# The sums of the LayerNorm behind depthwise convolutions, moved from GpSimd to VectorE in a two-layer hybrid backbone

## Chip, cores and metric

The kernel runs on 1 core of one Trainium2 chip. The metric is the device time of one execution in microseconds, from the first to the last instruction with what lies around them; several executions are taken and the median is shown. The profile is of one further execution.

## What is computed

Two layers, each with three branches over 1024 latent tokens and 256 context tokens of width 1024: windowed attention, a Conformer convolution, and a bidirectional gated recurrence. Every branch is gated, projected, merged and normalised. The change touches the convolution branch and, by a reservation of buffers, the attention. Cut to these:

```python
def layer_norm(x):
    mu = jnp.mean(x, -1, keepdims=True)
    var = jnp.mean(jnp.square(x - mu), -1, keepdims=True)
    return (x - mu) * lax.rsqrt(var + LN_EPS)

def conformer_conv(u, dw_w, dw_b, ln_g, ln_b):
    a, g = jnp.split(u, 2, axis=-1)
    y = a * jax.nn.sigmoid(g)
    y = depthwise_conv(y, dw_w, dw_b, (15, 15))      # 31 taps, one filter per channel, 512 channels
    y = layer_norm(y) * ln_g + ln_b                  # over the 512 channels
    return jax.nn.silu(y)
```

In attention, queries of a block of 128 tokens see their own and the neighbouring blocks of keys and the 256 context keys, with a learned sink per head.

## The kernel before

Channels lie on the 128 partitions and tokens along the free axis, so 512 channels are four tiles. Each layer has a first phase (`phase1`, line 525) with projections, convolution, recurrence and attention, and a second (`phase2`, line 1150) with the branch projections, the merge and the output. All large matrices are split into a rounded part and a remainder (hi and lo, as whi and wlo, ph and pl, qh and ql): ScalarE writes the first, VectorE the second, and TensorE multiplies three of the four combinations or, in attention, two.

The first phase is written as nine generators (line 1135): lru, att_values, att_scores, lru_in, lru_out, att_proj, att_out, conv and gates. A planner (class `Driver`, line 105) runs them in the order of estimated ready times and a priority table (line 44). It keeps its own clocks for TensorE, ScalarE and VectorE: every instruction given to these engines passes a `Meter` (line 52) that adds an estimated cost. GpSimd and the DMA queues have no clock in it. A generator yields the engine that its next step belongs to, an earliest time, and conditions such as room in a pool of buffers: `sl` holds 10 full-size slots, `hl_` 14 half-size tiles of 512 columns, `pl_` the use of PSUM. A step whose condition fails isn't taken. The gate projections (`gate_nt`, line 1093) need one tile of `hl_` for each step; they are long runs of matmuls that wait for nothing but weights and room, and so fill TensorE between steps of the others. The emitted program is put into each engine's queue by the framework's scheduler; on the chip each queue runs in order.

The convolution (`conv`, line 761) makes four accumulators of 31 taps each on VectorE and parks three of them in DRAM. Then, for each group of columns (layer 0: 256 context columns, 512, 512; layer 1: 512, 512), it loads them back (ab and acc2, line 804), adds the four tiles up on GpSimd into sm (lines 810 and 812), and sums over partitions with a matmul by a matrix of ones (line 816). VectorE subtracts the mean in place with four instructions that read that PSUM tile (line 820), ScalarE squares (line 824), GpSimd adds the squares up into sq (line 829), and a second matmul by ones gives the variance (line 831); root, reciprocal, scaling and the swish follow.

Attention is `att_scores` (line 945) and `att_values` (line 1034). For a block of 128 tokens and four heads, qh and ql are multiplied by the keys into PSUM; VectorE reads this with mask and maximum into P (in profiles CUSTOM_DVE_ANT_0, in the order ISA), ScalarE exponentiates, VectorE scales by the inverse sums es. TensorE transposes P in fours into pt, ScalarE and VectorE split pt into ph and pl, and two value products yp read these. A queue in order means that a value product on pl, and all matmuls behind it, wait until VectorE has come to that pl.

In `att_scores` the buffers of qh and ql are reserved (line 962) behind a yield that can pass control to other generators:

```python
yield ("act", hl_.room(3), at["proj"][2 * kv + 1])
qs[i] = load_q(kv, tl)
yield ("act", drv_.t["pe"] + LAG_Q[l])
...
hl_.take(2)
```

Of the kernel before, what the change touches and what calls it, by code (L numbers as in the profile page):

```python
# [12 lines left out]
ALU = mybir.AluOpType  # L13
# [176 lines left out]
def kernel(  # L190
# [7 lines left out]
    pool, sp = nc.gpsimd, nc.sync  # L198
    pe, act, dve = Meter(nc.tensor, pe_cost), Meter(nc.scalar, act_cost), Meter(nc.vector, dve_cost)
# [22 lines left out]
    def psum(n=512, name="ps"):  # L222
        return PM.tile([128, n], F32, tag="mm", name=name, bufs=4)
# [122 lines left out]
    def wroom(n=1):  # L346
        return lambda: wlive[0] + n <= NW

    def wcols(src, o):
        return Wt(src[:, o:o + 128].rearrange("(k p) n -> p k n", p=128), KD, 128)  # L350
# [171 lines left out]
    def both(*conds):  # L522
        return lambda: all(c() for c in conds)

    def phase1(l, R, RH):
# [5 lines left out]
        sl, hl_, pl_ = Pool_(NS), Pool_(NHF), Pool_(4)  # L531
        state = dict(lru=False, late=False)

        def slot(name, dt=F32):
            return R.tile([128, SLOT], dt, tag="s", name=name, bufs=NS)

        def half(name, dt=F32):
            return RH.tile([128, 512], dt, tag="h", name=name, bufs=NHF)
# [222 lines left out]
        def conv():  # L761
            for cc in range(4):
                yield ("pe", both(wroom(), sl.room(2)))
                sl.take(2)
                wg = wcols(w_in[l], O_U + BW + cc * 128)
                u = slot("u")
                if not last:
                    pool.memset(u[:, 0:15], 0.0)
                pool.memset(u[:, 15 + C:UL], 0.0)
                pool.memset(u[:, UL + S:UL + S + 15], 0.0)  # L770
                uo = lambda nt: u[:, 15:15 + C] if nt[0] == 0 else u[:, UL + nt[1] - C:UL + nt[1] - C + nt[2]]

                def evac_g(ps, nt):
                    act.activation(out=uo(nt), in_=ps, func=AF.Tanh, scale=0.5)

                def evac_a(ps, nt):
                    dve.scalar_tensor_tensor(out=uo(nt), in0=uo(nt), scalar=1.0, in1=ps, op0=ALU.add, op1=ALU.mult)

                for nt in full:
                    yield from gemm_nt(wg, nt, evac_g)  # L780
                wg.free()
                yield ("pe", wroom())
                wa = wcols(w_in[l], O_U + cc * 128)
                for nt in full:
                    yield from gemm_nt(wa, nt, evac_a)
                wa.free()
                acc = slot("acc")
                tap = lambda k: cwt[l][:, k * 4 + cc:k * 4 + cc + 1]
                yield "dve"
                dve.tensor_scalar(out=acc[:, QA:QE], in0=u[:, QA:QE], scalar1=tap(0),  # L790
                                  scalar2=p[:, P_CB + cc:P_CB + cc + 1], op0=ALU.mult, op1=ALU.add)
                for k in range(1, CK):
                    dve.scalar_tensor_tensor(out=acc[:, QA:QE], in0=u[:, QA + k:QE + k], scalar=tap(k),
                                             in1=acc[:, QA:QE], op0=ALU.mult, op1=ALU.add)
                    if k % 2 == 0 and k < CK - 1:
                        yield "dve"
                if cc < 3:
                    sp.dma_start(out=acc_d[cc][:, QA:QE], in_=acc[:, QA:QE])
                    sl.give(2)
            for nt in full:  # L800
                o, n = 0 if nt[0] == 0 else QL + nt[1] - C, nt[2]
                yield ("act", hl_.room(LH))
                hl_.take(LH)
                ab, a2 = slot("ab"), half("acc2")
                accs = [ab[:, 0:n], ab[:, 512:512 + n], a2[:, 0:n], acc[:, o:o + n]]
                for cc in range(3):
                    sp.dma_start(out=accs[cc], in_=acc_d[cc][:, o:o + n])
                yield ("dve", max(drv_.t["pe"], drv_.t["dve"]) + LAG_CONV[l])
                rstd, sm = half("rstd")[:, 0:n], half("sm")[:, 0:n]
                pool.tensor_tensor(out=sm, in0=accs[0], in1=accs[1], op=ALU.add)  # L810
                for cc in (2, 3):
                    pool.tensor_tensor(out=sm, in0=sm, in1=accs[cc], op=ALU.add)
                yield ("pe", lambda: pl_.used < 3)
                pl_.take()
                ps = psum()
                pe.matmul(out=ps[:, 0:n], lhsT=ones_f, rhs=sm, start=True, stop=True)
                sm = None
                for cc in range(4):
                    yield "dve"
                    dve.scalar_tensor_tensor(out=accs[cc], in0=ps[:, 0:n], scalar=-1.0 / BW, in1=accs[cc], op0=ALU.mult,  # L820
                                             op1=ALU.add)
                    yield "act"
                    sq = half("sq")[:, 0:n]
                    act.activation(out=sq, in_=accs[cc], func=AF.Square)
                    if sm is None:
                        sm = sq
                    else:
                        yield "dve"
                        pool.tensor_tensor(out=sm, in0=sm, in1=sq, op=ALU.add)
                yield "pe"  # L830
                pe.matmul(out=ps[:, 0:n], lhsT=ones_f, rhs=sm, start=True, stop=True)
                yield "act"
                act.activation(out=rstd, in_=ps[:, 0:n], func=AF.Sqrt, scale=1.0 / BW, bias=epsc)
                pl_.give()
                yield "dve"
                dve.reciprocal(out=rstd, in_=rstd)
                for cc in range(4):
                    yield "dve"
                    v = accs[cc]
                    dve.tensor_tensor(out=v, in0=v, in1=rstd, op=ALU.mult)  # L840
                    yield "act"
                    th = half("thc")[:, 0:n]
                    act.activation(out=th, in_=v, func=AF.Tanh, scale=d[:, 40 + cc:41 + cc], bias=d[:, 44 + cc:45 + cc])
                    act.activation(out=v, in_=v, func=AF.Identity, scale=p[:, P_CG + cc:P_CG + cc + 1],
                                   bias=p[:, P_CLB + cc:P_CLB + cc + 1])
                    yield "dve"
                    dve.scalar_tensor_tensor(out=v, in0=th, scalar=1.0, in1=v, op0=ALU.add, op1=ALU.mult)
                    sp.dma_start(out=acc_d[cc][:, o:o + n], in_=v)
                hl_.give(LH)
            sl.give(2)  # L850

            def get(nt):
                o, n = 0 if nt[0] == 0 else QL + nt[1] - C, nt[2]
                y = half("yc")
                sp.dma_start(out=y[:, 0:n], in_=acc_d[cc][:, o:o + n])
                return y[:, 0:n]

            for cc in range(4):
                yield from gating(1, cc, get, 0.5)
# [76 lines left out]
        def load_q(kv, tl):  # L936
            hl_.take()
            qd = half("qd")
            q3 = qd.rearrange("p (h t) -> p h t", t=128)
            for dh in range(2):  # L940
                sp.dma_start(out=q3[64 * dh:64 * dh + 64], in_=q_d[kv * 256:kv * 256 + 256, tl * 128:tl * 128 + 128].rearrange(
                    "(h p) t -> p h t", p=64))
            return qd

        def att_scores():

            qs = {}
            for i, (kv, tl) in enumerate(blocks):
# [7 lines left out]
                if i not in qs:  # L956
                    yield ("act", hl_.room(3), at["proj"][2 * kv + 1])
                    qs[i] = load_q(kv, tl)
                    yield ("act", drv_.t["pe"] + LAG_Q[l])
                else:  # L960
                    yield ("act", hl_.room(2))
                hl_.take(2)
                ks = at["ks"][kv]
                qh, ql = half("qh", F32R), half("ql", F32R)
                split(qs.pop(i), qh, ql)
# [139 lines left out]
        def gates():  # L1105
# [27 lines left out]
            assert not todo  # L1133

        drv_.run([lru(), att_values(), att_scores(), lru_in(), lru_out(), att_proj(), att_out(), conv(), gates()], PRIO[l])
        assert wlive[0] == 0 and sl.used == 0 and hl_.used == 0 and pl_.used == 0

# [334 lines left out]
```

## Time and profile before

| | |
|---|---|
| median of 3 runs | 2308.1 us (2306.67 to 2308.55) |
| the profiled execution | 2302.58 us |
| its span, first to last instruction | 2300.8 us |
| mean granted TensorE clock | 0.991 |
| TensorE busy | 2246.2 us (98%) |
| VectorE busy | 1681.3 us (73%) |
| ScalarE busy | 1004.4 us (44%) |
| GpSimd busy | 86.0 us (4%) |

In the profile PE is TensorE's matmuls, PEld its weight loads, DVE is VectorE, ACT ScalarE, POOL GpSimd and SP SyncE, which issues most DMAs. All instructions to metered engines are recorded by one line, 73, so they are told apart by their tiles: out<-in. A timeline row gives start, duration, engine and instruction, and in brackets how long the engine stood idle before it and what it waited for. Durations of neighbours overlap; the distance from one start to the next is what an instruction costs its queue.

### The profile page before, as it was taken

How to read it: one execution, taken by the hardware profiler on the slowest of the kernel's cores; microseconds unless marked ns; L12 is line 12 of the kernel's file. 1: busy time of each engine (PE TensorE's matmuls, PEld its weight loads, DVE VectorE, ACT ScalarE, POOL GpSimd, SP SyncE). 2: the span in 40 equal slices, each digit the busy share in tenths (PEclk: the TensorE clock that was granted, in tenths of full speed). 3: DMA queues.
4: the chain of work that ended last, by engine and by line, in shares of the span. 5: the costliest groups of instructions: out<-in, count | busy, mean ns of one | idle time of the engine just before them, and what ended most of it. 6: DMA issues, size and time to landing. Idle time of an engine off the chain costs nothing.

```text
span 2300.8 us, 29975 instructions
## 1 busy us (share of the span) xinstructions
PE 2246.2 (98%) x11344; PEld 1870.3 (81%) x11344; DVE 1681.3 (73%) x2453; ACT 1004.4 (44%) x1642; POOL 86.0 (4%) x140
## 2 busy tenths in 40 slices
PE   7999999999999999999999999999999999999998
PEld 2888888888888887888888788888888878878886
DVE  5579967868959875544678749879778797755767
ACT  4555563245444575421132544665243446642110
POOL 1000000000000111000001100000000011000002
PEclk8999999999999999999999999999999999999999
DMA  7223323433334232555561312224433234337532
GB/s 277 76 74 101 115 74 126 143 111 110 98 109 140 80 117 88 191 167 174 147 220 65 103 55 79 76 82 139 136 96 106 83 115 134 123 132 228 162 126 92
DMA packets 270945, 279.90 MB, mean 122 GB/s; under 512 B 19768, under 2 KB 199888, under 8 KB 270800
## 3 DMA queue, kind: packets, MB, share of 16 engines
q1 hardware_dynamic: 242288, 226.06, 31.5%
q10 hardware_dynamic: 28512, 51.92, 6.4%
q8 instruction: 89, 1.46, 0.3%
q14 instruction: 56, 0.46, 0.1%
HBM read 203.04 MB, written 74.88 MB: 121 GB/s over the span
## 4 chain that ended last, share of the span: by engine, by line
PE 91%; DVE 3%; ACT 3%; DMA 2%; issue 1%; POOLq 0%; SPq 0%; POOL 0%; DVEq 0%; ACTq 0%
PE ps L73 84%; PE yp L73 3%; PE pt L73 2%; PE pa L73 1%; ACT whi L73 0%; DMA raw<-in_w_ada_dram 0%; DVE acc L73 0%; DVE wlo L73 0%; DVE pl L73 0%; DVE P L73 0%; PE p L73 0%; DVE xp L73 0%; DMA raw<-in_w_in_dram 0%; ACT hf L73 0%; DMA yst<-yd 0%
## 5 line engine op out<-in xcount | busy, mean ns | idle before, releaser
L73 PE MATMUL ps<-hlhi,whi 128*128 128x512 f32 x1728 | 681.0, 395 | 2.8 <-DVE pl L73 1.5
L73 PE MATMUL ps<-hllo,whi 128*128 128x512 f32 x1728 | 677.2, 392 | 0.0
L73 PE MATMUL ps<-hlhi,wlo 128*128 128x512 f32 x1728 | 676.6, 392 | 0.0
L73 PEld LDWEIGHTS ps<-hlhi,wlo 128*128 128x128 f32 x1728 | 325.5, 188 | 67.8 <-issue 0.4
L73 PEld LDWEIGHTS ps<-hlhi,whi 128*128 128x128 f32 x1728 | 326.2, 189 | 66.6 <-DVE pl L73 2.8
L73 PEld LDWEIGHTS ps<-hllo,whi 128*128 128x128 f32 x1728 | 326.0, 189 | 61.8 <-issue 0.2
L73 DVE SCALAR_TENSOR_TENSOR acc<-u,cwt,acc 128x1296 f32<-128x1296 f32 (+1 forms) x240 | 341.8, 1424 | 2.2
L73 ACT ACTIVATE whi<-raw 128x1024 fp32r<-128x1024 f32 x180 | 190.1, 1058 | 336.7 <-PE ps L73 303.0
L73 DVE TENSOR_TENSOR wlo<-raw,whi 128x1024 fp32r<-128x1024 f32 x180 | 220.5, 1225 | 97.4 <-ACT whi L73 94.3
L73 PE MATMUL ps<-yy,whi 128*128 128x512 f32 (+1 forms) x960 | 271.5, 368 | 2.2 <-DVE m L73 2.2
L73 PEld LDWEIGHTS ps<-yy,whi 128*128 128x128 f32 x960 | 173.7, 188 | 32.7 <-DVE m L73 2.4
L73 PE MATMUL ps<-yy,wlo 128*128 128x512 f32 (+1 forms) x480 | 176.5, 368 | 0.0
L73 ACT ACTIVATE ph<-pt 128x512 fp32r<-128x512 f32 x160 | 94.2, 593 | 140.2 <-PE pt L73 138.4
L73 DVE TENSOR_TENSOR pl<-pt,ph 128x512 fp32r<-128x512 f32 x160 | 109.3, 686 | 54.5 <-ACT ph L73 52.9
L73 PE MATMUL ps<-hchi,whi 128*128 128x256 f32 x480 | 135.9, 283 | 1.2 <-DVE pl L73 0.4
L73 PE MATMUL ps<-hchi,wlo 128*128 128x256 f32 x480 | 135.5, 282 | 1.0 <-DVE wlo L73 1.0
L73 ACT ACTIVATE P<-P,nm 128x640 f32<-128x640 f32 (+1 forms) x128 | 101.9, 798 | 75.2 <-DVE nm L73 74.9
L73 PE MATMUL ps<-hclo,whi 128*128 128x256 f32 x480 | 134.7, 281 | 0.0
L73 DVE CUSTOM_DVE_ANT_0 P<-ps,m_mid,nsink 128x640 f32<-128x640 f32 (+1 forms) x112 | 93.4, 859 | 42.6 <-PE ps L73 41.1
L73 ACT ACTIVATE tg<-ps,drv 128x512 f32<-128x512 f32 (+1 forms) x120 | 76.5, 638 | 69.0 <-PE ps L73 68.4
L73 PEld LDWEIGHTS ps<-yy,wlo 128*128 128x128 f32 x480 | 90.5, 188 | 15.1
L73 PE MATMUL pt<-ident,P 128*128 128x128 f32 x640 | 97.5, 273 | 2.9 <-DVE pl L73 1.4
(205 smaller groups left out, 3397.9 us busy)
## 6 DMA issues: line engine op xcount, KB each, us to landing
raw<-in_w_in_dram SPq DMA_DIRECT2D x60, 512.0 KB
raw<-in_w_ada_dram SPq DMA_DIRECT2D x48, 512.0 KB
raw<-in_w_gate_dram SPq DMA_DIRECT2D x48, 512.0 KB
th<-tg ACTq DMA_DIRECT2D x96, 256.0 KB
thl<-th SPq DMA_DIRECT2D x96, 256.0 KB
yd<-gs ACTq DMA_DIRECT2D x48, 256.0 KB
yst<-yd SPq DMA_DIRECT2D x48, 256.0 KB
raw<-in_w_branch_dram SPq DMA_DIRECT2D x24, 512.0 KB
```

What stands on the lines that cost most here:

```text
L73: return f(*a, **k)
```

## The change

The three adds of the accumulators and the three adds of squares of each group are issued on VectorE instead of GpSimd. VectorE's instructions are metered, so the planner's clock for VectorE now counts them. In att_scores the two half-size buffers are reserved before the wait behind the load of queries, no longer after it.

```diff
--- before.py
+++ after.py
@@ -807,9 +807,9 @@
                     sp.dma_start(out=accs[cc], in_=acc_d[cc][:, o:o + n])
                 yield ("dve", max(drv_.t["pe"], drv_.t["dve"]) + LAG_CONV[l])
                 rstd, sm = half("rstd")[:, 0:n], half("sm")[:, 0:n]
-                pool.tensor_tensor(out=sm, in0=accs[0], in1=accs[1], op=ALU.add)
+                dve.tensor_tensor(out=sm, in0=accs[0], in1=accs[1], op=ALU.add)
                 for cc in (2, 3):
-                    pool.tensor_tensor(out=sm, in0=sm, in1=accs[cc], op=ALU.add)
+                    dve.tensor_tensor(out=sm, in0=sm, in1=accs[cc], op=ALU.add)
                 yield ("pe", lambda: pl_.used < 3)
                 pl_.take()
                 ps = psum()
@@ -826,7 +826,7 @@
                         sm = sq
                     else:
                         yield "dve"
-                        pool.tensor_tensor(out=sm, in0=sm, in1=sq, op=ALU.add)
+                        dve.tensor_tensor(out=sm, in0=sm, in1=sq, op=ALU.add)
                 yield "pe"
                 pe.matmul(out=ps[:, 0:n], lhsT=ones_f, rhs=sm, start=True, stop=True)
                 yield "act"
@@ -956,10 +956,11 @@
                 if i not in qs:
                     yield ("act", hl_.room(3), at["proj"][2 * kv + 1])
                     qs[i] = load_q(kv, tl)
+                    hl_.take(2)
                     yield ("act", drv_.t["pe"] + LAG_Q[l])
                 else:
                     yield ("act", hl_.room(2))
-                hl_.take(2)
+                    hl_.take(2)
                 ks = at["ks"][kv]
                 qh, ql = half("qh", F32R), half("ql", F32R)
                 split(qs.pop(i), qh, ql)
```

The change moves instructions, because the planner chooses anew from the first of these adds on. Up to there TensorE's order is the same. `ps<-sm,ones_f` is the matmul of the sums, `hlhi`, `hllo`, `whi` and `wlo` make projections, `pt` transposes, `ks` scores, `yp` value products.

TensorE, layer 0, around the second group's sum, before:

```order
L73 MATMUL ps<-hlhi,wlo 128x512
L73 MATMUL yp<-ph,vs 128x512
L73 MATMUL yp<-pl,vs 128x512
L73 MATMUL ps<-sm,ones_f 128x512
L73 MATMUL yp<-ph,vs 128x512
L73 MATMUL yp<-pl,vs 128x512
L73 MATMUL ps<-hlhi,whi 128x512
```

Here 19 projection matmuls follow in a row. With the change, the same place:

```order
L73 MATMUL ps<-hlhi,wlo 128x512
L73 MATMUL ps<-sm,ones_f 128x512
L73 MATMUL pt<-ident,P 128x128 x4
L73 MATMUL ps_7800<-ks,qh 128x384
L73 MATMUL ps_7800<-ks,ql 128x384
L73 MATMUL ps_7800<-ks,qh 128x256
L73 MATMUL ps_7800<-ks,ql 128x256
L73 MATMUL ps_7806<-ks,qh 128x384
L73 MATMUL ps_7806<-ks,ql 128x384
L73 MATMUL ps_7806<-ks,qh 128x256
L73 MATMUL ps_7806<-ks,ql 128x256
L73 MATMUL pt<-ident,P 128x128 x4
```

Behind it stand three more rounds of two value products and four transposes, eight scores on the next queries and a value product, and only then projections again. The projections between the sum and the attention's steps have moved.

VectorE, the same place with the change, directly behind the four subtractions of the mean (sq is the add of squares):

```order
L73 ISA P,nm_7713<-ps_7800,m_mid,nsink 128x640
L73 ISA nm_7713 128x1
L73 ISA P,nm_7713<-ps_7806,m_mid,nsink 128x640
L73 ISA nm_7713 128x1
L73 TENSOR_TENSOR pl<-pt,ph 128x512 x2
L73 TENSOR_TENSOR sq<-sq 128x512
L73 TENSOR_TENSOR es<-nm_7713,sink 128x4
L73 TENSOR_TENSOR pl<-pt,ph 128x512
L73 TENSOR_TENSOR es<-es,sm_7715 128x4
L73 RECIPROCAL es<-es 128x4
L73 TENSOR_SCALAR P<-P,es 128x640 x3
L73 TENSOR_TENSOR ql<-qd,qh 128x512
```

All pl that the value products read, and the ql that the next scores read, stand behind the subtractions and the two conversions to P; an add of squares stands between them.

TensorE, layer 1, around the second group's sum, before:

```order
L73 MATMUL yp<-ph,vs 128x512
L73 MATMUL yp<-pl,vs 128x512
L73 MATMUL ps<-sm,ones_f 128x512
L73 MATMUL yp<-ph,vs 128x512
L73 MATMUL ps_16659<-ks,qh 128x384
L73 MATMUL ps_16659<-ks,ql 128x384
L73 MATMUL ps_16659<-ks,qh 128x256
L73 MATMUL ps_16659<-ks,ql 128x256
L73 MATMUL ps<-hlhi,whi 128x512
```

Here 14 projection matmuls follow. With the change:

```order
L73 MATMUL ps<-hlhi,whi 128x512
L73 MATMUL ps<-sm,ones_f 128x512
L73 MATMUL pt<-ident,P 128x128 x4
L73 MATMUL ps<-hllo,whi 128x512
L73 MATMUL ps<-hlhi,wlo 128x512
L73 MATMUL ps<-hlhi,whi 128x512
L73 MATMUL ps<-hllo,whi 128x512
L73 MATMUL ps<-hlhi,wlo 128x512
L73 MATMUL pt<-ident,P 128x128 x4
L73 MATMUL yp<-ph,vs 128x512
L73 MATMUL yp<-pl,vs 128x512
L73 MATMUL yp<-ph,vs 128x512
```

Five projection matmuls stand between the sum and the first value products (one is left of the row that begins with the sum), and none between these and two further blocks of transposes, scores and products. On GpSimd the 30 adds are gone from the order, and what is left there keeps its order.

## Rows read from the trace of the kernel before

**Rows 1.** Page, busy time by engine: us (share of the span) xinstructions.
```profile
PE 2246.2 (98%) x11344; PEld 1870.3 (81%) x11344; DVE 1681.3 (73%) x2453; ACT 1004.4 (44%) x1642; POOL 86.0 (4%) x140
```

**Rows 2.** Windows: us, busy time and (xinstructions) by engine, PEclk, DMA share, GB/s.
```profile
763.00:835.00 72.00, 68.63 (x376) 58.68 (x375) 54.59 (x105) 45.71 (x91) 6.80 (x6) 0.95 0.33 101
835.00:898.00 63.00, 62.18 (x347) 52.74 (x345) 42.28 (x82) 41.87 (x81) 8.44 (x6) 1.00 0.32 99
1855.00:1905.00 50.00, 47.59 (x233) 38.88 (x233) 43.87 (x56) 28.37 (x48) 8.35 (x6) 1.00 0.34 106
1905.00:1945.00 40.00, 40.00 (x196) 33.04 (x195) 28.54 (x49) 26.00 (x47) 7.76 (x6) 1.00 0.39 122
```

**Rows 3.** Tiles sm and sq, GpSimd: count, ns min/median/max, first and last start.
```profile
L810 POOL TENSOR_TENSOR sm<-ab x5: 1287/1294/1476, 770.5 to 1914.7; 128x512 f32<-128x512 f32 x4, 128x256 f32<-128x256 f32 x1
...
L829 POOL TENSOR_TENSOR sq<-sq x15: 728/1295/1625, 790.2 to 1934.7; 128x512 f32<-128x512 f32 x12, 128x256 f32<-128x256 f32 x3
```

**Rows 4.** Groups by form, VectorE: xcount, busy us, mean ns, idle before, releasers.
```profile
L73 DVE TENSOR_TENSOR wlo<-raw,whi 128x1024 fp32r<-128x1024 f32 x180 | 220.5, 1225 | 97.4 <-ACT whi L73 94.3 <-PE yp L73 2.6
...
L73 DVE TENSOR_TENSOR m<-m,thl 128x512 f32<-128x512 f32 x64 | 44.1, 689 | 1.3
```

**Rows 5.** Timeline, VectorE beside GpSimd's adds: start us, us, what [idle before <-releaser].
```profile
771.66 0.37 DVE L73 TENSOR_TENSOR es<-nm,sink 128x4 f32<-128x4 f32 x1
...
793.17 1.22 DVE L73 TENSOR_TENSOR ql<-qd,qh 128x512 fp32r<-128x512 f32 x1
...
1935.44 0.56 DVE L73 TENSOR_TENSOR es<-es,sm 128x4 f32<-128x4 f32 x1 [0.81 <-ACT es L73]
```

**Rows 6.** Timeline, layer 0, third group of the LayerNorm, from its sum's matmul.
```profile
910.34 1.02 PE L73 MATMUL ps<-sm,ones_f 128*128 128x512 f32 x2
...
911.20 0.60 PE L73 MATMUL pt<-ident,P 128*128 128x128 f32 x4
...
912.23 1.29 DVE L73 SCALAR_TENSOR_TENSOR ab<-ps,ab 128x512 f32<-128x512 f32 x2
...
914.63 0.68 DVE L73 TENSOR_TENSOR pl<-pt,ph 128x512 fp32r<-128x512 f32 x1
...
915.36 0.80 PE L73 MATMUL yp<-ph,vs 128*128 128x512 f32 x1 [2.39 <-DVE pl L73]
```

**Rows 7.** Timeline, TensorE alone, ahead of the second group's sum.
```profile
843.69 0.33 PE L73 MATMUL ps<-ks,qh 128*128 128x384 f32 x1
...
844.87 0.60 PE L73 MATMUL pt<-ident,P 128*128 128x128 f32 x4
845.23 0.48 PE L73 MATMUL ps<-hlhi,whi 128*128 128x512 f32 x1
...
846.93 0.39 PE L73 MATMUL yp<-pl,vs 128*128 128x512 f32 x1
847.16 1.02 PE L73 MATMUL ps<-sm,ones_f 128*128 128x512 f32 x2
```

**Rows 8.** Timeline, VectorE's attention steps around the first group.
```profile
785.58 0.87 DVE L73 CUSTOM_DVE_ANT_0 P<-ps,m_mid,nsink 128x640 f32<-128x640 f32 x1
...
786.38 0.69 DVE L73 TENSOR_TENSOR pl<-pt,ph 128x512 fp32r<-128x512 f32 x1
...
791.78 1.48 DVE L73 TENSOR_SCALAR P<-P,es 128x640 f32<-128x640 f32 x3
```

**Rows 9.** Windows ahead of and in the two falls of the clock.
```profile
785.00:792.00 7.00, 4.96 (x27) 3.67 (x26) 6.96 (x17) 4.84 (x12) 0.85 (x1) 1.00 0.23 74
792.20:799.00 6.80, 5.83 (x18) 4.64 (x17) 4.56 (x9) 4.59 (x10) 1.72 (x2) 0.50 0.11 41
915.00:918.50 3.50, 3.14 (x9) 2.58 (x10) 1.40 (x3) 2.70 (x6) 3.34 (x3) 0.51 0.21 77
```

**Rows 10.** Timeline, tail of layer 1's attention, TensorE.
```profile
2042.26 0.50 PE L73 MATMUL yp<-ph,vs 128*128 128x512 f32 x1 [1.48 <-ACT ph L73]
```

**Rows 11.** Tile view of ab, the loads of the accumulators.
```profile
L807 SPq DMA_DIRECT2D ab<-acc x10: 333/422/531, 733.1 to 1902.6; - x10
```

## The prediction

> **What bounds the kernel now.** I read the engines' busy times first: TensorE is busy 2246.2 of the 2300.8 us, VectorE 1681.3, GpSimd 86.0 [rows 1]. So a time can fall only where TensorE stands idle or runs at its lower clock, and rises by every idle stretch that is added. The second view is the table of windows around the five places where the LayerNorm behind the convolutions runs (one group of 256 columns and two of 512 in layer 0, two of 512 in layer 1) [rows 2]. The reader should see that TensorE is nearly full although the LayerNorm runs there: 68.63 of 72 us around the first group, 62.18 of 63 around the second, 47.59 of 50 and 40.00 of 40 in layer 1. Third, the timeline of the places where it is not full: there matmuls wait, one instruction at a time, for VectorE's queue.
>
> **Part 1, the adds themselves.** GpSimd loses 30 adds, six in each of the five groups, 1.29 us each at 512 columns [rows 3]. VectorE gains the same 30: 24 at 0.69 us, which is what its own add of two tiles of this size takes [rows 4], and 6 of half the width, at about half: 16.6 + 2 = 18.6 us. Something comes back. While GpSimd adds, VectorE instructions that read two SBUF tiles are long: ql takes 1.22 us at 793.17 where it should take 0.69, and a four-column es 0.37 and 0.56 where 0.15 is usual [rows 5]. I count 15 such instructions, the first and the last of them in these rows; together they lose 9.7 us. The net load is +9 us, on an engine that has some 600 us free. If it all lay beside other work it would cost nothing; if all of it held up TensorE, 9 us. Neither happens evenly; the order decides.
>
> The Trainium skill (SBUF — State Buffer, Who interferes with whom) says that a VectorE instruction with two SBUF inputs contends with a GpSimd instruction that reads SBUF, and that the later one fully blocks. The stretched ql agrees. By that rule alone the change repays about half of its own price, and where a stretched instruction held TensorE it gains; that is the first rival.
>
> **Part 2, the order.** VectorE's time is counted by the kernel's own planner, GpSimd's is not, so the whole order behind the first sum is drawn anew. The second hunk also reserves two half-size buffers earlier, in which gate projections would have to find room. The order shows the result: behind the matmul of the sums (S below), 19 projection matmuls followed after two value products in the second group of layer 0; now there is none until the attention block is done. Such matmuls are the cover under which VectorE subtracts the mean; without them TensorE waits.
>
> How dear that is the third group of layer 0 shows, where it is so already. S starts at 910.34 and takes 0.86; the four subtractions start at 912.23 and end when pl starts at 914.63, so 0.60 each; the value product waits 2.39 us for pl [rows 6].
>
> Other prices are start to start. On TensorE: eight score matmuls 1.18 (843.69 to 844.87), four transposes 0.36, one value product or projection matmul 0.23 [rows 7]. On VectorE: scores to P 0.80 (785.58 to 786.38), scaling three P 1.4, pl, ql or an add of 512 columns 0.60 as the subtractions, small es 0.15, wlo at most 1.2 [rows 4, 6, 8].
>
> *Place A, layer 0, second group.* VectorE can begin 1.0 us after the start of S (0.86 and a hop): four subtractions 2.4, two P 1.6, two pl 1.2, one add of squares 0.6, es 0.15, pl 0.6, es and reciprocal 0.3, three P 1.4, ql 0.6: the scores on ql start 9.9 us after S. TensorE's own work until then: S 0.86, five times four transposes 1.8, eight scores 1.18, two more 0.3, six value products 1.4, together 5.5. Idle: 4.4 us. Before: nothing that the window of 62.18 in 63 shows but 0.8 in all [rows 2]. The moved add is 0.6 of the 4.4; the lost cover is the rest.
>
> *Place B, layer 1, second group.* From S: 1.0, three subtractions 1.8, three P 1.4, the fourth subtraction 0.6, pl 0.6, wlo 1.2, gating 0.6, pl and ql 1.2, the add of squares 0.6, gating 0.6, two pl 1.2, last product 0.2: 11.0. TensorE's work: 0.86 + five fours of transposes 1.8 + five projection matmuls 1.15 + eight scores 1.18 + eight products 1.84 = 6.8. Idle 4.2 us; before 40.00 of 40 busy, so 0 [rows 2].
>
> *Place C, layer 1, first group.* Now S stands behind the last add, which stands behind the conversion of the scores just made: S waits about 0.8. Behind S come eight transposes and a value product that needs pl, behind P, yt, es and four subtractions: 4.85 from S, against 1.8 of TensorE's work, 3.0 idle; the third block waits 0.9 behind two adds of squares and three P. Together 4.7 instead of the 2.4 of 50 there now [rows 2]: +2.3.
>
> *Place D, layer 0, first group.* The last add now stands behind P and a gating step, so S waits 2.2, and pl behind the subtractions costs 1.8: 4.0 instead of 2.0 (7.00 less 4.96) and 1.0 (6.80 less 5.83) [rows 9]: +1.0. The third group of layer 0 has S in front of eight transposes before and after: 0.
>
> *What goes.* The tail of layer 1 has stretches of transposes and products alone; at an ending block TensorE waits 1.48 [rows 10]. By the order one such end is covered now: -1.5. The 0.8 of the second group's window is redrawn: -0.8.
>
> *The clock.* After the idle 2.04 of 785 to 792 TensorE is granted 0.50 (1.2 of 2.4 GHz) for 6.8 us, after the 2.39 at 915 it has 0.51 for 3.5 us [rows 6, 9]. Half of that is lost: 3.4 and 1.75. A, B and C are idle stretches as long as these. Bounds: none falls, 0; all three for 6.8 us, +10.2. I take two short ones, +3.5, nearest to the one behind S at 915.
>
> DMAs and queues: the same transfers are issued on SP, in another order; in these windows no matmul waits on one, so 0, with the cover that ab's loads are issued at 1902.6 for an add of 1914.7 [rows 3, 11]. GpSimd's rest (memsets, small powers) keeps its order.
>
> **Sum.** 4.4 + 4.2 + 2.3 + 1.0 - 1.5 - 0.8 + 3.5 = +13.1 us. The profiled execution took 2302.58 us (span 2300.8), so 2315.7 for such a one; the runs' median is 2308.1, 5.5 above it, and the forecast is made on that: **2321 us**. Without the clock and with A and B half as long it is 2313; with all clock falls 2328.
>
> **Rivals.**
> *Faster, by the lock.* Around 790 TensorE waits behind a stretched es and ql. Without GpSimd's adds 0.5 of ql, 0.2 to 0.4 of each es go; with TensorE idle less there, the 6.8 us at half clock may not come either: about 2 + 3.4, and 1.5 of the tail: 2301. It decides if pl reaches the head of VectorE's queue before the transposes end. For it: the 9.7 us of stretched instructions. Against: place D's longer queue ahead of S. 0.11.
> *No change.* VectorE arrives at each S ahead of TensorE, adds and subtractions fit into its idle time, and the waits that come replace those that go: 2308, within 4. For it: VectorE is busy 42.28 of 63 and 28.54 of 40 us around the second groups [rows 2]. Against: what counts is the queue behind S. 0.17.
> *Slower still, by a blocked queue.* GpSimd could wait for a free sum tile or a loaded accumulator at no cost; VectorE's queue is in order, and everything behind it waits too. Two such waits of 4 us would give 2329. Against: the loads stand 12 us ahead. 0.10.
> *The change not in force* is excluded: the order has the adds on VectorE, none on GpSimd.
>
> **How the numbers follow.** Forecast 0.62, the rivals 0.10, 0.17, 0.11. A measurement can tell about 0.2%, 4.6 us. Faster is the first rival, 0.11; same the second, 0.17; slower 0.72. The forecast's own range is 2312 to 2329; the range of 8 in 10 reaches down into the unchanged case, 2307 to 2331, and leaves out most of the faster case and the end of the blocked one.
>
> **What would show it.** Right: in the windows of the second groups TensorE loses some 4 us, value products and scores there wait for pl and ql, the granted clock is under 1.00 in one or two more of the windows, ql is back at 0.69, VectorE's busy time is about 9 us up, GpSimd's 40 down. Wrong: those windows stay full, or an S waits for its sum by several us.

## The result, and the profile after

The changed kernel takes **2321.19 us** in the median of 4 runs (2320.23 to 2324.76), the kernel before, run beside it, 2307.39 (2305.5 to 2308.55, 4 runs): ratio 1.007, 95% interval 1.0058 to 1.0081. The medians differ by 13.8 us; by the interval of the ratio it is 13.4 to 18.7. Of the two profiled executions, the one of before lies 4.8 us under its kernel's median and the one of after 1.0 under its own; their spans, 2300.8 and 2318.4 us, therefore differ by 17.6.

The page of the changed kernel, busy time by engine, to be held beside [rows 1]:

```profile
PE 2256.4 (97%) x11344; PEld 1876.1 (81%) x11344; DVE 1690.1 (73%) x2483; ACT 1005.5 (43%) x1642; POOL 46.3 (2%) x110
```

VectorE has 30 instructions more and is busy 8.8 us longer, GpSimd 39.7 us shorter. The busy time of TensorE rose by 10.2 us with the same 11344 matmuls. It is at the lower clock for 13.0 us more in this execution than in that of before (55.9 against 42.9 us over the whole span), half of which, 6.5 us, explains most of it. The tiles sm and ql on VectorE: count, ns min/median/max, first and last start.

```profile
L73 DVE TENSOR_TENSOR sm<-sm,acc x10: 419/688/693, 788.9 to 1933.0; 128x512 f32<-128x512 f32 x8, 128x256 f32<-128x256 f32 x2
L73 DVE TENSOR_TENSOR sm<-ab x5: 416/682/686, 786.4 to 1930.8; 128x512 f32<-128x512 f32 x4, 128x256 f32<-128x256 f32 x1
...
L73 DVE TENSOR_TENSOR ql<-qd,qh x36: 628/686/694, 446.6 to 2017.5; 128x512 fp32r<-128x512 f32 x36
```

An add takes 0.68 to 0.69 us at 512 columns, and no ql is longer than 0.694 us any more: what [rows 5] showed as stretched is gone. Next the four windows of [rows 2], 1 us later in layer 0 and 8 us later in layer 1, since the attention of each layer begins about that much later; same columns.

```profile
764.00:836.00 72.00, 65.67 (x365) 56.45 (x364) 54.66 (x114) 46.33 (x92) 0.00 (x0) 0.98 0.32 100
836.00:899.00 63.00, 60.33 (x331) 50.79 (x330) 44.87 (x85) 40.94 (x78) 0.00 (x0) 0.97 0.31 97
1863.00:1913.00 50.00, 46.43 (x222) 37.44 (x221) 41.64 (x60) 25.28 (x44) 0.00 (x0) 0.97 0.27 84
1913.00:1953.00 40.00, 37.45 (x180) 30.97 (x180) 32.39 (x63) 26.82 (x52) 0.00 (x0) 0.96 0.44 139
```

Each window has lost TensorE time: 2.96, 1.85, 1.16 and 2.55 us against [rows 2], 8.5 together, and the three that had the full clock are now at 0.96 or 0.97. Where it is lost, in the timeline of TensorE (the prediction's places D, A, C and B in order of time, and, second, one that it did not have; the bracket is the idle time before and what ended it):

```profile
790.51 1.19 PE L73 MATMUL ps<-sm,ones_f 128*128 128x256 f32 x2 [2.47 <-DVE sm L73]
...
814.89 0.50 PE L73 MATMUL yp<-ph,vs 128*128 128x512 f32 x1 [2.82 <-DVE pl L73]
...
857.42 0.51 PE L73 MATMUL yp<-pl,vs 128*128 128x512 f32 x1 [2.35 <-DVE pl L73]
...
1891.74 0.51 PE L73 MATMUL yp<-pl,vs 128*128 128x512 f32 x1 [1.97 <-DVE pl L73]
...
1942.95 0.50 PE L73 MATMUL yp<-ph,vs 128*128 128x512 f32 x1 [2.52 <-DVE pl L73]
```

And what VectorE does while TensorE waits at 857.42 (place A):

```profile
852.68 1.29 DVE L73 SCALAR_TENSOR_TENSOR ab<-ps,ab 128x512 f32<-128x512 f32 x2
853.88 1.28 DVE L73 SCALAR_TENSOR_TENSOR acc<-ps,acc 128x512 f32<-128x512 f32 x2
855.08 0.88 DVE L73 CUSTOM_DVE_ANT_0 P<-ps,m_mid,nsink 128x640 f32<-128x640 f32 x1
...
855.88 0.88 DVE L73 CUSTOM_DVE_ANT_0 P<-ps,m_mid,nsink 128x640 f32<-128x640 f32 x1
...
856.68 1.28 DVE L73 TENSOR_TENSOR pl<-pt,ph 128x512 fp32r<-128x512 f32 x2
```

Four subtractions, two blocks of scores and only then pl; no add of the change stands in that chain. The clock, in windows laid on its falls (PEclk is the figure after the last bracket of counts):

```profile
858.20:861.60 3.40, 3.40 (x15) 2.73 (x13) 2.94 (x9) 2.25 (x5) 0.00 (x0) 0.51 0.00 0
...
1039.10:1042.50 3.40, 3.38 (x8) 2.71 (x9) 1.85 (x3) 0.63 (x1) 0.00 (x0) 0.51 0.79 246
1892.50:1895.90 3.40, 2.91 (x10) 2.09 (x9) 3.40 (x8) 2.23 (x4) 0.00 (x0) 0.50 0.26 75
1943.70:1947.10 3.40, 3.37 (x13) 2.58 (x13) 3.40 (x7) 0.60 (x1) 0.00 (x0) 0.50 0.52 151
1998.30:2001.70 3.40, 3.40 (x9) 2.65 (x9) 3.40 (x9) 1.75 (x3) 0.00 (x0) 0.50 0.31 109
```

None of the five is in the trace of before. The first stands behind place A, the third and fourth behind C and B, the second behind a wait of 2.84 us for the merge and the fifth behind the 1.31 us at 1997.13. In each TensorE is at the lower level (1.2 of 2.4 GHz) for 3.4 us.

### The profile page after: what moved, and what is told of

It is laid out like the page before. It is cut to its first block, busy times and chain, and to the rows that moved or that the text cites. A ratio compares the mean times of both kernels' runs of the same rounds, so it can differ in the third digit from the quotient of the medians.

```text
span 2318.4 us, 29945 instructions
## 1 busy us (share of the span) xinstructions
PE 2256.4 (97%) x11344; PEld 1876.1 (81%) x11344; DVE 1690.1 (73%) x2483; ACT 1005.5 (43%) x1642; POOL 46.3 (2%) x110
## 4 chain that ended last, share of the span: by engine, by line
PE 89%; DVE 5%; ACT 2%; DMA 2%; issue 1%; SPq 0%; POOLq 0%; POOL 0%; ACTq 0%; DVEq 0%
PE ps L73 82%; PE yp L73 3%; PE pt L73 2%; PE pa L73 1%; DVE P L73 1%; DVE acc L73 1%; DVE pl L73 1%; DMA qd<-qd 1%; DMA yst<-yd 1%; DVE wlo L73 1%; ACT whi L73 0%; DMA raw<-in_w_ada_dram 0%; PE p L73 0%; DVE xp L73 0%; ACT hf L73 0%
```

## The experiments

Two causes are mixed in the change: VectorE's queue is longer by the adds (**load**), and, because the planner counts VectorE's time, the order of everything behind the first sum is another one (**order**). The reason given in the prediction was the order: gate projections no longer stand behind the matmul of the sums S, as cover. The first four kernels take the two apart. Each shows its edit against the change or against the kernel before; medians and ratios are against the kernel before run in the same session. Behind them stands a table that answers for all where the time lies.

**E1. The adds on VectorE, not counted.** `dve` is the engine with the planner's meter, `nc.vector` the bare engine; the other two adds alike:

```diff
-                dve.tensor_tensor(out=sm, in0=accs[0], in1=accs[1], op=ALU.add)
+                nc.vector.tensor_tensor(out=sm, in0=accs[0], in1=accs[1], op=ALU.add)
```

> The adds are on VectorE as in the change, but issued beside the planner's count of VectorE's time, so the planner draws nearly the order of the kernel before: 24, 43 and 70 projection matmuls stand again behind the matmul of the sums in the second group of layer 0 and in the two groups of layer 1. Theory 1, the order (the change's loss is the cover that the new order takes from behind these matmuls): 2308 us, 2303 to 2312, with the windows of both second groups full again, TensorE idle in the two layers' LayerNorm windows about 18 us as before (9.5 + 8.95) and not 26, and VectorE still some 9 us busier than before. Theory 2, the load (VectorE's queue is longer by the adds, and matmuls wait for it whatever the order): 2317 to 2324 us, idle stays at 23 to 26.

Measured: 2310.48 us against 2306.91, ratio 1.0015 (1.0005 to 1.0024): +3.6 us of the 13.8, inside what the order theory expected. VectorE is busy 1688.6 us, the load is there in full, and TensorE's order is nearly that of before: compared one against the other, 67 of the 11344 matmuls stand elsewhere, with the change 956. The profiled execution took 2305.71 us, among the shortest of a spread from 2305.59 to 2312.5. Its windows at the times of [rows 2], first, second and last:

```profile
763.00:835.00 72.00, 65.48 (x374) 56.58 (x374) 54.12 (x111) 46.21 (x91) 0.00 (x0) 1.00 0.33 100
835.00:898.00 63.00, 62.49 (x348) 53.16 (x347) 46.04 (x89) 42.50 (x81) 0.00 (x0) 1.00 0.33 99
...
1905.00:1945.00 40.00, 39.50 (x191) 32.41 (x190) 29.15 (x54) 25.21 (x46) 0.00 (x0) 1.00 0.40 126
```

Both second groups are full again; the first group is not (65.48 against 68.63), because its S waits for the sum:

```profile
789.38 0.67 PE L73 MATMUL ps<-sm,ones_f 128*128 128x256 f32 x2 [2.47 <-DVE sm L812]
```

What E1 leaves out is the new order, so about 10 of the 13.8 us go with the order and a rest with the load.

**E2. Every add twice.** E1, with each add done once more into a tile that is written over later (the other adds alike):

```diff
+                nc.vector.tensor_tensor(out=rstd, in0=accs[0], in1=accs[1], op=ALU.add)
                 nc.vector.tensor_tensor(out=sm, in0=accs[0], in1=accs[1], op=ALU.add)
```

> As the run without the count, but each of the 30 adds is done a second time into a tile that is written over later, so VectorE is busy 18.6 us more (30 adds more), in nearly the same order. Theory 1, the order: 0 to 4 us over the run without the count, since cover hides the adds in three groups of five and only the first and third group of layer 0 have them bare. Theory 2, the load: 9 to 18 us over it.

Measured: 2321.22 us, ratio 1.0063 (1.005 to 1.0077): 10.7 us over E1. The order theory expected 0 to 4, so as the only cause it falls; the load theory's 9 to 18 holds. Load costs too, where nothing covers it. The waits of TensorE in layer 0 are those of E1, longer, and new ones behind later groups:

```profile
791.57 1.19 PE L73 MATMUL ps<-sm,ones_f 128*128 128x256 f32 x2 [3.47 <-DVE sm L814]
...
867.80 0.39 PE L73 MATMUL ps<-hchi,whi 128*128 128x256 f32 x1 [2.05 <-ACT rstd L73]
```

In layer 1, where 45 and 66 projection matmuls stand behind the two S, its attention phase is only 0.8 us longer than in E1.

**E3. The adds on GpSimd, counted as if on VectorE.** The reverse of E1:

```diff
+class Charged:
...
+    def tensor_tensor(self, **k):
+        n = k["out"].shape[1]
+        self.meter.t += self.meter.cost("tensor_tensor", n, k)
+        return self.eng.tensor_tensor(**k)
...
+    dadd = Charged(pool, dve)
...
-                dve.tensor_tensor(out=sm, in0=accs[0], in1=accs[1], op=ALU.add)
+                dadd.tensor_tensor(out=sm, in0=accs[0], in1=accs[1], op=ALU.add)
```

> The reverse: the adds stay on GpSimd, but the planner counts each of them on VectorE as the change does, so the order is drawn anew and no projection matmul stands behind any of the five matmuls of the sums. Theory 1, the order: 2321 us, 2316 to 2328 (GpSimd's adds are 1.29 and not 0.69 us each, which the lost cover no longer hides, so it may be a few us above the change). Theory 2, the load: 2306 to 2310 us as before, since VectorE has not one add more.

Measured: 2319.9 us, ratio 1.0059 (1.0044 to 1.0073). Not one add more is on VectorE, TensorE's order is that of the change but for 68 matmuls, and the kernel is 13.0 us slower than before. The load theory's 2306 to 2310 falls. The two prices do not add up to the change's (3.6 and 13.0 against 13.8): GpSimd's adds are longer, and waits of one kind replace those of the other. The wait of place A is there to the hundredth, now at the full clock, and two more follow it:

```profile
850.11 1.02 PE L73 MATMUL ps<-sm,ones_f 128*128 128x512 f32 x2
...
855.98 0.50 PE L73 MATMUL yp<-pl,vs 128*128 128x512 f32 x1 [2.35 <-DVE pl L73]
...
858.64 0.51 PE L73 MATMUL yp<-ph,vs 128*128 128x512 f32 x1 [0.82 <-ACT ph L73]
859.41 0.50 PE L73 MATMUL yp<-pl,vs 128*128 128x512 f32 x1 [0.26 <-DVE pl L73]
...
860.42 0.28 PE L73 MATMUL ps<-ks,ql 128*128 128x256 f32 x1
```

The same stretch of the change, from the matmul of the sums to the first scores on the new ql, has only the first of these waits and is no shorter (10.6 us against 10.3):

```profile
851.57 1.02 PE L73 MATMUL ps<-sm,ones_f 128*128 128x512 f32 x2
...
862.18 0.38 PE L73 MATMUL ps<-ks,ql 128*128 128x256 f32 x1
```

**E4. E1 with another due time.** `LAG_CONV = (20.0, 10.0)` becomes `(18.0, 10.0)`, which moves the cover in layer 0 from the second group to the third.

> The run without the count, with the first sum of layer 0 due 18 us after the planner's clock and not 20 (LAG_CONV). By the order the second group of layer 0 loses its cover and the third gains 24 projection matmuls; layer 1 keeps 43 and 70. Theory 1, the order: the idle stretch behind the third group's matmul (2.39 us before) goes and one of some 2 us comes in the second: within 4 us of the run without the count, either way. Theory 2, the load: the same as that run within 2 us, at 2317 to 2324.

Measured: 2313.36 us, ratio 1.0035 (1.0022 to 1.0048), 2.9 us over E1 and so inside what the order theory allowed; the load theory's 2317 to 2324 falls. The second group's value products now wait 1.31 and 2.15 us; behind the third group's sum the 2.39 are gone, but 1.40 and 0.78 are left. Layer 0's attention phase is 6.3 us longer in its trace than in E1's and layer 1's the same.

**E5 and E6. The change in full, with due times that put cover back.** One number (E5) or two (E6) for each group of columns, read by the line `... + LAG_CONV[l][gi])`:

```diff
-LAG_CONV = (20.0, 10.0)
+LAG_CONV = ((20.0, 20.0, 20.0), (6.0, 10.0))
...
-LAG_CONV = (20.0, 10.0)
+LAG_CONV = ((20.0, 20.0, 24.0), (6.0, 10.0))
```

> The change in full (adds on VectorE, counted there), with one number more: the first sum of layer 1 is due 6 us after the planner's clock and not 10. By the order layer 0 stays word for word as in the change, and in layer 1 24 and 60 projection matmuls stand again behind the two matmuls of the sums (0 and 5 in the change). Theory 1, cover: the attention phase of layer 1, which was 9.0 us longer than before under the change, is 2 to 4 longer, so 2311 to 2318 in all, likeliest 2315; VectorE is as busy as under the change. Theory 2, the load on VectorE: 2319 to 2324 as under the change.

> The change in full, with the first sum of layer 1 due after 6 us and the one of layer 0's third group after 24 us: by the order 24, 24, 43 and 60 projection matmuls stand behind the matmuls of the sums of all groups but the first (before: 24, 0, 43, 68; change: 0, 0, 0, 5). Theory 1, cover: the price of the bare load, some 3.5 us, less the idle stretch and clock fall behind the third group (2.4 + 1.7): 2303 to 2310, likeliest 2307. Theory 2, the load on VectorE: 2317 to 2324, because not one add less is on VectorE than under the change.

The numbers of the order in both expectations are wrong: in the kernels that ran, 46 and 94 projection matmuls stand behind the two S of layer 1, and none behind those of layer 0. Measured: E5 2328.12 us, ratio 1.0097 (1.0083 to 1.011); E6 2324.27, ratio 1.0082 (1.0068 to 1.0095). Both theories miss E5, and the cover theory misses E6 too (2303 to 2310). E6 lies at the upper end of what the load theory said, but E3, without that load, is nearly as slow. The cover did its work where it was put: at the two S of layer 1 TensorE waits 0.75 us in all, for the sum, where the change has the waits of C and B. But the same order leaves another place bare, later in the phase:

```profile
1977.54 0.90 PE L73 MATMUL pt<-ident,P 128*128 128x128 f32 x3 [6.06 <-ACT P L73]
```

The values of a block stand there five matmuls behind its last scores, TensorE waits 6.06 us for P, and from 2.1 us into that wait it has half its clock for 6.8 us. Cover behind S alone is therefore not the measure of an order; the idle of the whole phase is.

**E7. The kernel before, with cover for the third group too.** Adds on GpSimd; `LAG_CONV` as above with `((20.0, 20.0, 16.0), (10.0, 10.0))`, which redraws TensorE's order around that group and leaves it nearly everywhere else. E7 and E8 also have the change's earlier reservation of buffers, which by itself moves no instruction.

> The kernel before (adds on GpSimd), with the sum of layer 0's third group due after 16 us and not 20; all else of the order is the same, and 24 projection matmuls now stand behind that group's matmul of the sums. Theory 1, cover: the 2.39 us of idle behind it and the fall of the clock after it go: 2301 to 2305. Rival: the wait moves to the next place where VectorE's queue is long: 2306 to 2309 as before.

Measured: **2301.42 us** against 2305.87, ratio 0.9983 (0.9975 to 0.9992), 4.5 us faster than the kernel before and the lowest median of the study. What [rows 6] and [rows 9] showed as 2.39 us of idle and a fall of the clock is this now, matmul against matmul behind S, at the full clock:

```profile
905.61 1.02 PE L73 MATMUL ps<-sm,ones_f 128*128 128x512 f32 x2
906.07 0.79 PE L73 MATMUL ps<-hlhi,whi 128*128 128x512 f32 x1
906.70 0.39 PE L73 MATMUL ps<-hllo,whi 128*128 128x512 f32 x1
```

**E8. The kernel before, with the last group's sum due earlier.** As E7, with `((20.0, 20.0, 20.0), (10.0, 4.0))`.

> The kernel before (adds on GpSimd, not one on VectorE), with the sum of layer 1's second group due after 4 us and not 10; layer 0 and the first group of layer 1 keep their order, and the 68 projection matmuls behind the last matmul of the sums are gone. Theory 1, cover: the place that the change made idle (2.5 us and a fall of the clock) shows 2 to 4 us of idle here too, and the run takes 2309 to 2315. Theory 2, the load on VectorE: 2305 to 2309 as before.

Measured: 2314.51 us, ratio 1.0042 (1.0029 to 1.0054): +8.6 us with no add on VectorE. But the order is not the expected one: 50 projection matmuls stand between S and the second matmul by ones (47 in the kernel before), so S is not bare, and TensorE waits there only 0.35 us. Bare is the second matmul: the first value product follows it at once, where 21 projection matmuls stood ahead of it. There ScalarE does the root, with a load of function tables before it and one behind it (1.28 us each), ahead of ph:

```profile
1946.67 1.02 PE L73 MATMUL ps<-sq,ones_f 128*128 128x512 f32 x2
1948.47 0.50 PE L73 MATMUL yp<-ph,vs 128*128 128x512 f32 x1 [0.78 <-ACT rstd L73]
...
1950.87 0.71 PE L73 MATMUL yp<-ph,vs 128*128 128x512 f32 x1 [1.66 <-ACT ph L73]
```

The time lies in the cover theory's 2309 to 2315, but not by the wait that it named. Two falls of the clock, 3.4 us at 1951.0 and 6.8 us at 2053.4, do the rest in that layer.

**E9 to E11. E7's order with all, or half, of the adds on VectorE, not counted.** E9 moves all six adds of a group, E10 the three adds of squares, E11 the three of the sum:

```diff
-                        pool.tensor_tensor(out=sm, in0=sm, in1=sq, op=ALU.add)
+                        nc.vector.tensor_tensor(out=sm, in0=sm, in1=sq, op=ALU.add)
```

> All adds on VectorE as in the change, issued beside the planner's count (as in E1), and the third group of layer 0 due after 16 us (as in E7): by the order 24, 24, 43 and 70 projection matmuls stand behind the matmuls of the sums of the last four groups. If order and load are two prices that simply add, it is E7's 2301 plus the 3.5 us that E1 lost: 2303 to 2307, no slower than the kernel before, with every add of the change in place. Theory of the load alone: 2317 or more. If the load costs more where VectorE's queue now stands in front of cover: 2308 to 2312.

> E7's kernel with only the three adds of squares of each group on VectorE, beside the planner's count; the three adds that make the first sum stay on GpSimd. If the 3.5 us of E1 are the wait of the first matmul of the sums for VectorE's queue (2.5 and 0.7 us in E1's trace, which GpSimd does not have), this one costs nothing over E7: 2299 to 2303. If they are VectorE's queue behind the squares: 2303 to 2306.

> The other half: E7's kernel with only the three adds that make the first sum of each group on VectorE, beside the planner's count; the adds of squares stay on GpSimd. If the wait of the first matmul of the sums is what the load costs, the whole 3.5 us come here: 2303 to 2307, with TensorE idle about 2.5 us ahead of the first group's matmul. If it is the squares: 2299 to 2303.

Measured against 2306.34: E9 2305.38 (ratio 1.0001, 0.9991 to 1.001), E10 2303.45 (0.9987, 0.9978 to 0.9995), E11 2305.25 (0.9996, 0.9987 to 1.0005). E9 has every add of the change on VectorE and is no slower than the kernel before, 15.8 us under the change. Against E7, which has the same cover, it is 4.0 us slower, so order and load add up here as expected. The halves lean the way expected, the sums costing more; but E10 lies on the border of its two cases, and E10 and E11 differ by less than their intervals, so this is not settled by the times. The traces show where the sums cost: S of the first group waits 2.47 us for its sum in E9 and E11, and in E10 it is not among the waits.

**Where the time lies, in all of them.** For the attention phase of each layer (in layer 0 from the first value product to the first matmul of the merge, in layer 1 from the first value product to the last), worked out from the trace: its length, the sum of TensorE's gaps between matmuls, and the time at the lower clock (a part of which can lie within a wait), in us.

| kernel | layer 0: length, idle, low clock | layer 1: length, idle, low clock |
|---|---|---|
| before | 559.3, 13.2, 13.7 | 384.3, 9.0, 0 |
| change | 564.3, 16.8, 13.7 | 393.4, 11.9, 10.2 |
| E1 uncounted | 558.7, 15.6, 6.8 | 386.5, 9.3, 3.4 |
| E2 twice | 570.1, 20.3, 20.5 | 387.3, 8.9, 6.8 |
| E3 counted, GpSimd | 560.9, 15.7, 6.8 | 394.3, 13.5, 6.8 |
| E4 uncounted, 18 | 565.0, 16.9, 13.7 | 386.5, 9.3, 3.4 |
| E5 change, 6 | 567.9, 17.3, 20.5 | 397.6, 16.0, 13.7 |
| E6 change, 24 and 6 | 562.7, 16.3, 10.2 | 398.0, 16.0, 13.7 |
| E7 before, 16 | 555.9, 10.5, 10.2 | 384.5, 9.0, 0 |
| E8 before, 4 | 562.7, 14.7, 17.1 | 393.9, 12.3, 10.2 |
| E9 uncounted, 16 | 556.8, 14.9, 3.4 | 386.5, 9.3, 3.4 |
| E10 squares | 553.6, 9.2, 6.8 | 386.6, 9.4, 3.4 |
| E11 sums | 557.6, 14.9, 3.4 | 384.3, 8.9, 0 |

Length less idle less half the time at the lower clock is 539.3 to 541.9 in layer 0 and 374.8 to 377.3 in layer 1, for all thirteen. So within these phases the traces leave no third cause of any size: kernels differ by TensorE's idle and by the clock that follows it. In layer 1 the adds on VectorE cost at most 3.0 us (E1, E2, E9), and the counted order 9 to 14, whichever engine adds (change, E3, E5, E6). In layer 0 the two causes are not as clearly apart: TensorE's idle is 2.4 us longer with the load alone (E1), 2.5 with the order alone (E3) and 3.6 with both, and falls of the clock decide the rest. Each row of the table is one execution; where a fall of 3.4 or 6.8 us comes or stays away, a row moves by 1.7 or 3.4.

Outside the two phases the spans differ too: 1357.2 us before, 1360.7 with the change, 1364.4 in E3. Of the change's 3.5 us, 0.9 lie ahead of the first value product, and 2.2 between the layers, where the matmul that begins the merge waits longer (2.84 us against 2.21) and a fall of the clock follows it. That matmul waits 2.0 to 3.9 us in all thirteen, and a fall comes with it in eight, whatever the order.

## Why the prediction was right, and where its steps were not

The forecast was 2321 in 2307 to 2331, from +13.1 us; measured were 2321.19 and +13.8. The mechanism is shown: E3 has the new order without the load and is 13.0 us slower, E1 has the load without the new order and is 3.6 slower. That the number was met within a microsecond is luck: the terms below miss by more, in both directions, and the two profiled executions, for which the +13.1 were worked out, differ by 17.6.

- *Part 1 held.* Net load +9 on VectorE: +8.8. GpSimd minus 40: minus 39.7. ql is back at 0.69. Its bounds, nothing if the load lies beside other work and 9 us if all of it holds TensorE, take in what was measured: +3.6 in E1, and +4.0 from E7 to E9.
- *"The moved add is 0.6 of the 4.4; the lost cover is the rest"* held for place A: E3 has the same 2.35 us without the add, E1 has the add and no wait there.
- *The size of A and B was too large*: 4.4 and 4.2 of idle forecast; the waits are 2.35 and 2.52. VectorE's queue was sized well: from S to the scores on ql place A takes 10.6 us, 9.9 in the sum. TensorE's own work was not: at the full clock, in E3, it is 6.9 us there (10.3 less waits of 2.35, 0.82 and 0.26), 5.5 in the sum. And TensorE did not keep its pace: in place A all of 858.2 to 861.6 is busy, at half clock, so the later waits of the sum became slow work. *The clock term* has what these two lack: forecast +3.5 for two falls. Without the 13.7 us that both have at the start, the profiled execution of after is at the lower clock for 34.1 us up to the last value product, that of before for 20.5: 6.8 us lost by halves, toward the upper bound of 10.2, of which A, B and C have 5.1. Idle and clock were priced as two things that add, but an idle that the slow clock swallows was counted among the idle.
- *C* was forecast at +2.3 and is +1.2 in its window. *D* was forecast at +1.0 and is +3.0 in its window: S does wait, 2.47 us (2.2 in the sum), but the 2.82 us at 814.89 were not in the prediction. There a pl stands in VectorE's queue behind the scaling of the accumulators, three P and a wlo, the same pattern at a place that was not worked out. The fall of the clock at D is 3.4 us long now and was 6.8, which gives 1.7 us back.
- *The tail* lost one of its two 1.48 us waits, as forecast; against it stand 0.53 and 1.31 us at 1995 to 1997 and the fall at 1998.3, which were not forecast. The four windows' idle together is 8.5 us against the 11.1 of the forecast's terms for them (A, B, C, D, less the 0.8).
- *The signs.* In the windows of the second groups TensorE lost 1.85 and 2.55 us, not some 4; the clock is under 1.00 in three more of the windows, not in one or two.
- *The rivals.* The faster one fell: the stretched instructions did go, and E9, which keeps that gain and has cover behind four of the five sums, only just meets the time of before and lies 4.0 us over E7. Of a VectorE instruction with two SBUF inputs and a GpSimd instruction that reads SBUF, the Trainium skill (SBUF — State Buffer, Who interferes with whom) has the later one blocked. The trace agrees: no ql is over 0.694 us once GpSimd's adds are gone, and in E3, where they stay, the longest takes 1.78. But the lock did not set the sign; the order did. The unchanged case is E9, with an order that the change does not draw. The blocked queue did not come: none of the 30 adds waits for a loaded accumulator or a free sum tile in the changed kernel's trace.

Not settled: why the planner's order with the adds counted is worse than without. The four kernels with it (the change, E3, E5, E6) took 2319.9 to 2328.1 us; the planner's rules were not tried one by one. The second hunk by itself moves no instruction on any engine, so it was not run alone; the first without it leaves the planner short of half-size tiles, so that half was not tried either.

## To carry to other kernels

When an order is drawn by a planner that keeps an engine's clock, moving work to that engine changes two things; run the moved work uncounted, and the count without the work, before blaming the load. Read the price of an order from the whole phase's idle and its clock, not from one place: cover put back at one wait (E5) opened a dearer one elsewhere, and one number for one group (E7, 4.5 us) was worth as much as the engine of 30 adds (3.6 to 4.0). If the adds are to be on VectorE, E9 has them at the time of before; the best median found keeps them on GpSimd and covers the third group: 2301.42 us, with E10, which moves the squares alone, inside the noise of it (0.9987 against 0.9983 of the kernel before).

## What was not expected of the hardware

- A short wait can cost more than its length. Behind A, B, C and the wait of 2.84 us ahead of 1039.12 the clock of the changed kernel was at its lower level for 3.4 us each, which costs up to 1.7 us each time. It is not sure to come: the 2.82 us ahead of 814.89 and, in E1, the 2.47 us ahead of 789.38 were followed by no fall, the 3.47 us at the same matmul in E2 by one of 6.8 us. The wait for the merge was 2.35 us in E7, with a fall behind it, and 3.46 us in E4, with none.
- The lower clock hides waits. At place A the change, at half clock, shows one wait, and E3, at the full clock, three; yet from the end of the first wait to the scores on the next queries it is 4.03 us in the change and 4.12 in E3, which has one add less in VectorE's queue there. A fall in front of a queue that TensorE would wait for anyway cost next to nothing.
- Which engine holds TensorE within one group depends on which of its two matmuls by ones is bare: behind S it was VectorE's queue (1.97 to 2.52 us at A, B and C), behind the second one, in E8, ScalarE's root and its table loads (0.78 and 1.66 us).
